# Norms between sub-layers of a two-layer decoder: old root ahead of the residual add, quotient applied to products, transposes placed by hand

## The chip, the cores and the metric

The kernel runs on one core of a Trainium2 chip. The metric is device time in microseconds for one execution. Engines are named as in the profile: PE is TensorE (its weight loads are PEld), DVE is VectorE, ACT is ScalarE, POOL is GpSimd, SP is SyncE, which issues nearly all transfers. Each engine works through its instructions in a fixed order, and an instruction that waits holds up those behind it on the same engine.

## The reference: what is computed

Two decoder layers over 256 rows (tokens) of 1024 numbers, float32. Each layer has three sub-layers: a feed-forward part, a mixer (pooling in layer 0, dilated attention in layer 1), a second feed-forward part. Every sub-layer has a norm on its input and one on its output, ahead of the residual add:

```python
def rms_norm(x, gain):
    y = x * lax.rsqrt(jnp.mean(x * x, axis=-1, keepdims=True) + RMS_EPS) * gain

def swiglu(h, w_gate, w_up, w_down):
    return (jax.nn.silu(h @ w_gate) * (h @ w_up)) @ w_down

# for each layer, with its six gains g
f = swiglu(rms_norm(h, g[0]), w_gate[0], w_up[0], w_down[0])
h = h + 0.5 * rms_norm(f, g[1])
mix = mixer(rms_norm(h, g[2]))
h = h + rms_norm(mix, g[3])
f = swiglu(rms_norm(h, g[4]), w_gate[1], w_up[1], w_down[1])
h = h + 0.5 * rms_norm(f, g[5])
# behind layer 0: keys and values for layer 1, from a norm of h with a gain of its own
```

## The kernel before

**Tiles.** The 256 rows are two blocks of 128 (block 0 and block 1; `i` in the code). The residual stream `h[0]`, `h[1]` stays in SBUF. Every product in float32 is made of three: each operand is split into a rounded high part and the rest (`hl`: high on ACT, line 99 or 106; rest on DVE, line 100 or 107), and high x high, high x low and low x high are added up in PSUM (`proj_mm`, lines 129 to 141; `row_mm`, lines 143 to 150). A product of 512 columns is one PE instruction. The weights come from HBM as one stream in the order of use, 1 MB at a time; a "unit" is half of that once it is split.

**A feed-forward sub-layer** (`ffn`, lines 272 to 451) first takes the normed, transposed rows `aT` against the first 512 gate and 512 up columns: `acc_b`, for each block 24 products for the gate and 24 for the up (lines 395 to 400). Then come two `pair`s (lines 335 to 387), which make one column group with seven block products instead of eight, by sums of blocks (`Sums`, lines 210 to 245, holds those of the rows); of the four sums of weight blocks in each pair two are made on DVE (line 333) and two by accumulating transfers that POOL issues (line 331). Then a last group, and the down projection `acc_d` over 22 row groups of 128 (lines 433 to 450). The last six of these (`TAIL = 6`) are kept back, so that block 0 is finished first: its 36 products of the tail, then the join for block 0, then the 36 of block 1's tail (six units of six products), in whose shadow block 0's join runs. The pool mixer ends in the same way (`acc_w`, lines 617 to 629).

**The join between two sub-layers** is the class `Bound` (lines 453 to 480) in three steps, for each block:

- `first`: `post` (lines 181 to 195). ACT squares both halves of the output in PSUM and sums them (line 174), DVE adds the two sums (line 176), POOL takes the power -1/2 (line 178). DVE multiplies the output with its gain (line 188 or 190) and adds it, times the root, to `h` (line 193).
- `second`: `norm` (lines 250 to 261). The same again for the new `h`: squares (line 174), sum, root, the product with the next gain (line 255), and the scaling by the root, one half on DVE (line 256), one on ACT (line 258).
- `third`: `transposed` (lines 197 to 208): eight PE transposes (line 203, tiles `tp`), then two casts to the high part on ACT (line 205) and two subtractions on DVE (line 206) into `aT`. Where the next sub-layer has `Sums`, ACT copies the transposed rows (line 230) and DVE and ACT build the sums.

There are five such joins, in the profile `f` for the three behind a feed-forward part (f00, f01, f10) and `m` for the two behind a mixer (m0, m1): f00, m0, f01, f10, m1 in order of time. Behind f10 the next stage is the key projection (`kp`, lines 670 to 679), which reads other rows (`hk`, a norm of its own, lines 636 to 642), not the rows of this join. The kernel starts with a norm of x (lines 482 to 498).

**What sets the order.** Most of the order on each engine is made by a planner from estimated durations: an instruction that is written earlier goes first when, by the estimate, both could run. On PE too it chooses where among the products the transposes go. Within `tc.manual_schedule(engines=...)` the order on the named engines is that of the code. That holds for DVE and ACT at the start (line 485) and in the attention part, and for PE in the attention part (lines 782 to 830), where block 0's transposes are written at `go.third(0)` behind it. `tc.issue_after(ins)` lets the instructions of its block that run on the engine of `ins` come only behind `ins`.

Of the kernel before, what the change touches and what calls it, by code (L numbers as in the profile page):

```python
# [11 lines left out]
F32 = mybir.dt.float32  # L12
# [15 lines left out]
TAIL = 6  # L28
DMA_SUMS = (2, 3)
# [18 lines left out]
def trunk_kernel(ctx: ExitStack, tc: tile.TileContext, x, pos, gains, pscale, ws, wq, invf, amask, pmat, icnt, out):  # L48
# [76 lines left out]

    def mm(o, l, r, start, stop):
        nc.tensor.matmul(o, l, r, start=start, stop=stop)  # L127
# [42 lines left out]
    def rstd_of(halves, name):  # L170
        ss = st.tile([P, 2], F32, tag="ss", name=f"ss_{name}")
        for k in range(2):
            jk = sc1.tile([P, 512], BF16, tag="junk", bufs=1, name=f"jk_{name}{k}")
            nc.scalar.activation(jk, halves[k], AF.Square, scale=1.0 / 32.0, accum_out=ss[:, k : k + 1])
        ms = st.tile([P, 1], F32, tag="ms", name=f"ms_{name}")
        nc.vector.scalar_tensor_tensor(ms, ss[:, 0:1], EPS, ss[:, 1:2], op0=ALU.add, op1=ALU.add)
        rs = st.tile([P, 1], F32, tag="rs", name=f"rs_{name}")
        nc.gpsimd.tensor_tensor(rs, ms, nhalf, op=ALU.pow)
        return rs
# [67 lines left out]
    def row_rstd(i, name):  # L247
        return rstd_of([h[i][:, 0:512], h[i][:, 512:1024]], f"q{name}{i}")

    def norm(i, gain, name, rs=None, split=True):  # L250
        rs = row_rstd(i, name) if rs is None else rs
        y = sc4.tile([P, D], F32, tag="y", name=f"n_{name}{i}")
        for k in range(2):
            c = slice(k * 512, (k + 1) * 512)
            nc.vector.tensor_mul(y[:, c], h[i][:, c], gain[:, c])
        nc.vector.tensor_scalar_mul(y[:, 0:512], y[:, 0:512], rs)
        if split:
            nc.scalar.mul(y[:, 512:1024], y[:, 512:1024], rs)
        else:
            nc.vector.tensor_scalar_mul(y[:, 512:1024], y[:, 512:1024], rs)  # L260
        return y

    def pre(i, gain, aT, name):
        transposed(i, norm(i, gain, name), aT, name)
# [7 lines left out]
    def ffn(n, aT, sums, boundary, middle=None, late=None):  # L272
# [180 lines left out]
    class Bound:  # L453


        def __init__(self, n, post_idx, half, pre_idx, sums=False):
            self.n, self.half, self.idx = n, half, (post_idx, pre_idx)
            self.want, self.sums = sums, None

# [17 lines left out]
        def __call__(self, i, f):  # L477
            self.first(i, f)
            self.second(i)
            self.third(i)  # L480

    gpre = load_gain(0, "pre")
    aT = new_aT("x")
    sums = Sums("x")
    with tc.manual_schedule(engines={mybir.EngineType.DVE, mybir.EngineType.Activation}):
        y = norm(0, gpre, "x")
# [4 lines left out]
        rs = row_rstd(1, "x")  # L491
        load_raw(at=1, raw=raws[0])
        first_units += [parts(raws[0], 1, xy=True)]
        y = norm(1, gpre, "x", rs, False)
# [38 lines left out]
    go = Bound("f00", 1, True, 2)  # L533
# [3 lines left out]
    aT = go.aT  # L537
    go = Bound("m0", 3, False, 4, True)
# [16 lines left out]
    def u_proj(i, n):  # L555
        proj_mm(uu[i][n], aT, i, units[n * 4 : n * 4 + 4], 512)
        d = u_hl[i][:, :, n * 512 : (n + 1) * 512]
        nc.scalar.copy(d[:, 0], uu[i][n])
        nc.vector.tensor_sub(d[:, 1], uu[i][n], d[:, 0])
# [38 lines left out]
    u_proj(0, 1)  # L598
# [21 lines left out]
    for i in range(2):  # L620
# [5 lines left out]
        else:  # L626
            for k in range(8 - TAIL, 8):
                wout(k, i)
        go(i, f[i])

    prev, go = go, Bound("f01", 5, True, 6, True)
    ffn(1, prev.aT, prev.sums, go)
# [3 lines left out]
    def kv_input():  # L636
        kvgain = load_gain(12, "post")
        hk.append(new_aT("hk"))
        for i in range(2):
            with in_turn("dve"):  # L640
                y = norm(i, kvgain, "kv")
            transposed(i, y, hk[0], "kv")

    prev, go = go, Bound("f10", 7, True, 8)
    ffn(2, prev.aT, prev.sums, go, None, kv_input)
# [3 lines left out]
    aT = go.aT  # L649
    go = Bound("m1", 9, False, 10, True)  # L650
# [19 lines left out]
    for g in range(3):  # L670
        units = load_units(4, g % 2 == 0)
        for i in range(2):
            ps = gup.tile([P, 512], F32, tag="gu", name=f"kp{g}{i}")
            proj_mm(ps, hkT, i, units, 512)
# [107 lines left out]
    with tc.manual_schedule(engines={mybir.EngineType.PE}):  # L782
# [44 lines left out]
        go.second(0)  # L827
        o_proj(1, (2,))
        values(3, 1)
        o_proj(1, (3,))  # L830
# [13 lines left out]
    ffn(3, go.aT, go.sums, Finish())  # L844
# [117 lines left out]
```

## Time and profile before

| what | value |
|---|---|
| median of 3 runs | 984.6 us (982.15 to 986.87) |
| the profiled execution | 985.76 us |
| its span | 984.0 us |
| mean granted clock of TensorE | 0.986 |
| instructions | 12092 |
| moved from HBM over the span | 178.54 MB read, 183 GB/s |
| longest wait of PE for another engine | 3.8 us, at the start (`tp_x` for `n_x`) |

How to read it: the page gives the busy time of every engine, and the chain that ended last is followed back from the last instruction to what released each step. In a list of groups a row is line, engine, operation, output<-inputs, count, then busy time and the mean time of one in ns, then idle time of the engine just before. In a timeline a row is start and length in us, engine, line, operation, tiles, shape, count of merged instructions, and in brackets the idle time ahead and what ended it. In the busy times by stretch each engine has its busy us and its count of instructions, in the order PE, PEld, DVE, ACT, POOL, then the granted clock, the share of the transfers' engines and GB/s.

### The profile page before, as it was taken

How to read it: one execution, taken by the hardware profiler on the slowest of the kernel's cores; microseconds unless marked ns; L12 is line 12 of the kernel's file. 1: busy time of each engine (PE TensorE's matmuls, PEld its weight loads, DVE VectorE, ACT ScalarE, POOL GpSimd, SP SyncE). 2: the span in 40 equal slices, each digit the busy share in tenths (PEclk: the TensorE clock that was granted, in tenths of full speed). 3: DMA queues.
4: the chain of work that ended last, by engine and by line, in shares of the span. 5: the costliest groups of instructions: out<-in, count | busy, mean ns of one | idle time of the engine just before them, and what ended most of it. 6: DMA issues, size and time to landing. Idle time of an engine off the chain costs nothing.

```text
span 984.0 us, 12092 instructions
## 1 busy us (share of the span) xinstructions
PE 950.4 (97%) x4560; PEld 783.7 (80%) x4560; DVE 684.1 (70%) x771; ACT 542.9 (55%) x693; POOL 62.3 (6%) x66
## 2 busy tenths in 40 slices
PE   7999999999999999999999999999987899999997
PEld 6888788878788878877888888788976778887886
DVE  5979874577788886458887964785465587887642
ACT  6665753455657565347656743644345576665531
POOL 0000000000100000000000000100033310000000
PEclk8999999999999999999999999999999799999999
DMA  7886876475468687546687765564324236967721
GB/s 248 286 266 205 259 260 207 173 227 187 164 211 265 181 280 261 179 139 213 153 317 218 268 243 175 177 217 139 127 95 153 86 107 194 330 163 260 247 90 43
DMA packets 55898, 197.16 MB, mean 200 GB/s; under 512 B 7392, under 2 KB 7392, under 8 KB 53792
## 3 DMA queue, kind: packets, MB, share of 16 engines
q1 hardware_dynamic: 53456, 179.35, 52.2%
q0 software_dynamic: 2384, 17.04, 8.9%
q8 instruction: 36, 0.59, 0.2%
q14 instruction: 22, 0.18, 0.0%
HBM read 178.54 MB, written 1.05 MB: 183 GB/s over the span
## 4 chain that ended last, share of the span: by engine, by line
PE 74%; DVE 11%; ACT 5%; DMA 4%; issue 3%; POOL 2%; SPq 0%; POOLq 0%; DVEq 0%; ACTq 0%
PE acc_d L127 22%; PE g L127 12%; PE st L314 12%; PE u L127 7%; PE acc_b L127 6%; PE vp L127 3%; DVE hl L100 3%; PE kp L127 3%; DMA xy<-raw 2%; DVE hl_lo L107 2%; PE htp L295 2%; ACT hl L99 2%; PE qp L127 1%; DVE h L193 1%; PE acc_w L127 1%
## 5 line engine op out<-in xcount | busy, mean ns | idle before, releaser
L100 DVE TENSOR_TENSOR hl<-raw,hl 128x1024 fp32r<-128x1024 f32 x182 | 221.0, 1222 | 111.6 <-ACT hl L99 110.5
L99 ACT CAST hl<-raw 128x1024 fp32r<-128x1024 f32 x182 | 189.7, 1051 | 138.3 <-PE acc_d L127 103.3
L127 PE MATMUL acc_d<-hl,h 128*128 128x512 f32 x1056 | 243.5, 390 | 0.0
L127 PEld LDWEIGHTS acc_d<-hl,h 128*128 128x128 f32 x1056 | 197.3, 188 | 40.4
L107 DVE TENSOR_TENSOR hl_lo<-xy,hl_hi 128x2048 fp32r<-128x2048 f32 x40 | 91.6, 2291 | 48.6 <-ACT hl_hi L106 48.6
L107 DVE TENSOR_TENSOR hl_lo<-raw,hl_hi 128x2048 fp32r<-128x2048 f32 x48 | 109.4, 2285 | 15.6 <-ACT hl_hi L106 15.5
L106 ACT CAST hl_hi<-xy 128x2048 fp32r<-128x2048 f32 x40 | 76.5, 1913 | 64.0 <-DVE xy L333 29.7
L106 ACT CAST hl_hi<-raw 128x2048 fp32r<-128x2048 f32 x48 | 91.9, 1914 | 20.8 <-PE st L314 10.6
L127 PE MATMUL acc_b<-hl,aT_m 128*128 128x512 f32 x192 | 44.8, 392 | 0.3 <-ACT aT_m L205 0.3
L127 PEld LDWEIGHTS acc_b<-hl,aT_m 128*128 128x128 f32 x192 | 35.7, 188 | 8.3 <-ACT aT_m L205 0.8
L127 PE MATMUL g<-hl_hi,aT_m 128*128 128x512 f32 x128 | 41.9, 393 | 0.0
L127 PE MATMUL u<-hl_hi,aT_m 128*128 128x512 f32 x128 | 41.8, 393 | 0.0
L314 PE MATMUL st<-hl_hi,S_m 128*128 128x512 f32 x128 | 41.8, 393 | 0.0
L127 PE MATMUL qp<-hl,aT_f 128*128 128x384 f32 x192 | 38.9, 354 | 0.0
L297 ACT CAST h<-htp 128x512 fp32r<-128x512 f32 (+1 forms) x48 | 26.2, 548 | 20.0 <-PE htp L295 20.0
L127 PEld LDWEIGHTS qp<-hl,aT_f 128*128 128x128 f32 x192 | 34.8, 198 | 1.3 <-issue 0.8
L127 PE MATMUL kp<-hl,aT_hk 128*128 128x512 f32 x144 | 34.6, 394 | 0.0
L331 POOL DMA_DIRECT2D xy<-raw x16 | 14.1, 878 | 305.2 <-DVE xy L333 82.3
L127 PE MATMUL vp<-hl,aT_hk 128*128 128x512 f32 x144 | 33.1, 390 | 0.0
L314 PE MATMUL st<-hl_hi,aT_m 128*128 128x512 f32 x96 | 31.6, 393 | 1.3 <-ACT hl L99 0.9
L721 POOL TENSOR_SCALAR p<-p,rd 128x512 f32<-128x512 f32 x16 | 24.9, 1566 | 121.9 <-DVE rd L720 100.1
L298 DVE TENSOR_TENSOR h<-htp,h 128x512 fp32r<-128x512 f32 (+1 forms) x48 | 30.6, 640 | 1.1 <-ACT h L297 1.0
(246 smaller groups left out, 1596.4 us busy)
## 6 DMA issues: line engine op xcount, KB each, us to landing
raw<-in_ws SPq DMA_DIRECT2D x278, 512.0 KB, 4.8
xy<-in_ws SPq DMA_DIRECT2D x32, 512.0 KB, 6.8
xy<-raw POOLq DMA_DIRECT2D x16, 1024.0 KB, 8.1
rawq<-in_wq SPq DMA_DIRECT2D x8, 768.0 KB, 4.7
gain_post<-in_gains SPq DMA_DIRECT2D x14, 256.0 KB, 5.0
gain_pre<-in_gains SPq DMA_DIRECT2D x12, 256.0 KB, 6.1
rawpm<-in_pmat SPq DMA_DIRECT2D x2, 512.0 KB, 4.1
out_dram<-h SPq DMA_DIRECT2D x4, 256.0 KB, 2.1
```

Source lines behind the costliest of these rows:

```text
L99: nc.scalar.copy(hl[:, 0, :n], raw[:, k, :n])
L100: last["dve"] = nc.vector.tensor_sub(hl[:, 1, :n], raw[:, k, :n], hl[:, 0, :n])
L106: nc.scalar.copy(hi, raw)
L107: last["dve"] = nc.vector.tensor_sub(lo, raw, hi)
L127: nc.tensor.matmul(o, l, r, start=start, stop=stop)
L193: nc.vector.scalar_tensor_tensor(h[i][:, c], y[:, c], rs, h[i][:, c], op0=ALU.mult, op1=ALU.add)
L295: nc.tensor.transpose(tp[:, k], prod[c, i][:, k * P : (k + 1) * P], ident)
L297: nc.scalar.copy(d[:, 0], tp[:, :nt])
L298: nc.vector.tensor_sub(d[:, 1], tp[:, :nt], d[:, 0])
L314: nc.tensor.matmul(ps, a(z, k), u[v], start=start and k == 0 and n == 0, stop=k == 3 and n == 2, skip_group_check=not start,)
L331: nc.gpsimd.dma_start(dst, src, accum_op=ALU.add)
L721: nc.gpsimd.tensor_scalar_mul(p, p, rd)
```

## The change

The rows that are transposed are no longer fully normed. Let r be the inverse root of the rows at the join before (`old`) and h the rows behind the residual add. Now each half of h is, directly behind its own residual add (`post` calls `done`, here `scaled`), multiplied by r and by the next gain in one DVE instruction. These rows are transposed. The true inverse root of h is obtained beside it: with m the mean square of h, `q = (m r r)^(-1/2)` is the quotient of new and old root, and `r q` the new root for the next join. The quotient is a factor per row, so it is applied behind the products: as the scale of the gate's SiLU and as a factor in the up product (`ffn`), as the scale of the pool mixer's copies (`u_proj`), and into the rope tables of the queries once the keys are done. The key/value norm takes the kept root and makes none of its own.

`Bound.first` now holds the residual add and these rows, `second` the transposes, `third` the squares, the quotient and the sums. `second` and `third` are put on a list and run at a hand-set mark: for block 0 behind the fourth of the six units of block 1's tail (`TURN_0 = 3`), for block 1 in the next stage behind the first unit of its second half (`TURN_1 = 0`): in `ffn` the first up unit of block 0, in the pool mixer that of block 0's second half, in the key projection the first unit of block 1. In the attention part block 0's `second` is written behind `values(3, 1)`.

The diff, without the unchanged lines around and without what only passes names along:

```diff
+TURN_0, TURN_1 = 3, 0
...
+    waiting = []
     def mm(o, l, r, start, stop):
-        nc.tensor.matmul(o, l, r, start=start, stop=stop)
+        last["mm"] = nc.tensor.matmul(o, l, r, start=start, stop=stop)
+
+    def run_waiting():
+        while waiting:
+            with tc.issue_after(last["mm"].ins):
+                waiting.pop(0)()
...
-    def norm(i, gain, name, rs=None, split=True):
-        rs = row_rstd(i, name) if rs is None else rs
+    def norm(i, gain, name, rs):
         y = sc4.tile([P, D], F32, tag="y", name=f"n_{name}{i}")
         for k in range(2):
             c = slice(k * 512, (k + 1) * 512)
-            nc.vector.tensor_mul(y[:, c], h[i][:, c], gain[:, c])
-        nc.vector.tensor_scalar_mul(y[:, 0:512], y[:, 0:512], rs)
-        if split:
-            nc.scalar.mul(y[:, 512:1024], y[:, 512:1024], rs)
-        else:
-            nc.vector.tensor_scalar_mul(y[:, 512:1024], y[:, 512:1024], rs)
+            nc.vector.scalar_tensor_tensor(y[:, c], h[i][:, c], rs, gain[:, c], op0=ALU.mult, op1=ALU.mult)
         return y
...
         def gate(c, i, g):
-            nc.scalar.activation(act[c, i][:, :w], g, AF.Silu)
+            nc.scalar.activation(act[c, i][:, :w], g, AF.Silu, scale=1.0 if q is None else q[:, i : i + 1])
         def up(c, i, u):
-            nc.vector.tensor_mul(prod[c, i][:, :w], u, act[c, i][:, :w])
+            if q is None:
+                nc.vector.tensor_mul(prod[c, i][:, :w], u, act[c, i][:, :w])
+            else:
+                nc.vector.scalar_tensor_tensor(
+                    prod[c, i][:, :w], u, q[:, i : i + 1], act[c, i][:, :w], op0=ALU.mult, op1=ALU.mult
+                )
...
             if n > 0:
                 proj_mm(gu[i][0], aT, i, units[:4], 512)
-                proj_mm(gu[i][1], aT, i, units[4:], 512)
+                for j in range(4):
+                    proj_mm(gu[i][1], aT, i, units[4:], 512, only=j)
+                    if j == TURN_1:
+                        run_waiting()
...
                 for t in range(TAIL):
                     down(NF - TAIL + t, i, tail[t])
+                    if t == TURN_0:
+                        run_waiting()
             boundary(i, f[i])
...
         def first(self, i, f):
-            post(i, f, self.gpost, self.half, self.n)
+            self.y = []
+            def scaled(i, c):
+                if not self.y:
+                    self.y.append(sc4.tile([P, D], F32, tag="y", name=f"n_{self.n}{i}"))
+                nc.vector.scalar_tensor_tensor(
+                    self.y[0][:, c], h[i][:, c], self.old[:, i : i + 1], self.gpre[:, c], op0=ALU.mult, op1=ALU.mult
+                )
+            post(i, f, self.gpost, self.half, self.n, scaled)
         def second(self, i):
-            self.y = norm(i, self.gpre, self.n)
+            transposed(i, self.y[0], self.aT, self.n, self.sums)
         def third(self, i):
-            transposed(i, self.y, self.aT, self.n, self.sums)
+            z, old = slice(i, i + 1), self.old[:, i : i + 1]
+            ms = mean_square(h_halves(i), f"q{self.n}{i}")
+            nc.vector.scalar_tensor_tensor(ms, ms, old, old, op0=ALU.mult, op1=ALU.mult)
+            nc.gpsimd.tensor_tensor(self.q[:, z], ms, nhalf, op=ALU.pow)
+            nc.gpsimd.tensor_mul(self.r[:, z], self.q[:, z], old)
             if self.sums is not None:
                 self.sums.add(i)
         def __call__(self, i, f):
             self.first(i, f)
-            self.second(i)
-            self.third(i)
+            def rest():
+                self.second(i)
+                self.third(i)
+            waiting.append(rest)
...
+    for i in range(2):
+        for t in (ctab, stab):
+            nc.vector.tensor_scalar_mul(t[:, i], t[:, i], qu[:, i : i + 1])
...
         p_turn(3, 1)
-        go.second(0)
         o_proj(1, (2,))
         values(3, 1)
+        go.second(0)
         o_proj(1, (3,))
     go.third(0)
     go(1, acc_f[1])
```

More of the change, by code (lines that the diff above doesn't have):

```diff
@@ L485, in trunk_kernel @@
     with tc.manual_schedule(engines={mybir.EngineType.DVE, mybir.EngineType.Activation}):
[L486 removed]
+        y = norm(0, gpre, "x", rstd_of(h_halves(0), "qx0", rx[:, 0:1]))
         raws = [load_raw(at=0)]
@@ L553, in trunk_kernel, with u_proj @@
     uu = [acc_pair(f"u{i}") for i in range(2)]
-    def u_proj(i, n):
-        proj_mm(uu[i][n], aT, i, units[n * 4 : n * 4 + 4], 512)
+    def u_proj(i, n, turn=False):
+        for q in range(4):
+            proj_mm(uu[i][n], aT, i, units[n * 4 : n * 4 + 4], 512, only=q)
+            if turn and q == TURN_1:
+                run_waiting()
         d = u_hl[i][:, :, n * 512 : (n + 1) * 512]
-        nc.scalar.copy(d[:, 0], uu[i][n])
-        nc.vector.tensor_sub(d[:, 1], uu[i][n], d[:, 0])
+        nc.scalar.mul(d[:, 0], uu[i][n], qu[:, i : i + 1])
+        nc.vector.scalar_tensor_tensor(
+            d[:, 1], uu[i][n], qu[:, i : i + 1], d[:, 0].bitcast(F32), op0=ALU.mult, op1=ALU.subtract
+        )
     yT = [s8p.tile([P, 2, 4, S], F32R, tag="s8", name=f"yT{k}") for k in range(2)]
@@ L673, in trunk_kernel @@
             ps = gup.tile([P, 512], F32, tag="gu", name=f"kp{g}{i}")
-            proj_mm(ps, hkT, i, units, 512)
+            for q in range(4):
+                proj_mm(ps, hkT, i, units, 512, only=q)
+                if i == 1 and q == TURN_1:
+                    run_waiting()
             r = rope(ps, i, 8, f"k{g}{i}")
```

52 lines of the change are left out of this document (29 added, 23 removed).

## The prediction

> **What bounds the kernel now.** I read the page first: the busy shares and the chain that ended last.
>
> ```profile
> PE 950.4 (97%) x4560; PEld 783.7 (80%) x4560; DVE 684.1 (70%) x771; ACT 542.9 (55%) x693; POOL 62.3 (6%) x66
> PE 74%; DVE 11%; ACT 5%; DMA 4%; issue 3%; POOL 2%; SPq 0%; POOLq 0%; DVEq 0%; ACTq 0%
> ```
>
> TensorE (PE) is busy for 97% of the span and carries 74% of the chain. Its speed inside a stage comes from the chain in order of time, its spare room from the busy times by stretch: one feed-forward sub-layer, then two stretches around a join between sub-layers.
>
> ```profile
> 61.72 5.44 PE u L127 x24
> 20.00:190.00 170.00, 168.96 (x764) 139.29 (x765) 125.64 (x123) 95.35 (x96) 3.63 (x4) 1.00 0.74 243
> 190.00:212.00 22.00, 20.84 (x99) 16.51 (x98) 18.45 (x28) 14.42 (x27) 3.98 (x4) 1.00 0.61 187
> 434.00:458.00 24.00, 22.19 (x105) 17.60 (x104) 20.22 (x31) 18.73 (x38) 3.06 (x4) 1.00 0.39 132
> ```
>
> Twenty-four 512-column products take 5.44 us, so one slot is 0.227 us. From 20 to 190 us PE is busy for 168.96 of 170.00 us; around the joins it is 20.84 of 22.00 and 22.19 of 24.00, and DVE is at 18.45 and 20.22. So the joins hold the idle time. PE's own waits say for what:
>
> ```profile
> PE tp_f L203 <- DVE n_f L256: 3.8, 6, 0.8
> PE tp_m L203 <- DVE n_m L256: 1.9, 3, 0.8
> PE acc_b L127 <- ACT aT_m L205: 0.3, 1, 0.3
> PE acc_u L127 <- ACT aT_f L205: 0.3, 1, 0.3
> PE acc_b L127 <- ACT aT_f L205: 0.3, 1, 0.3
> L127 PE MATMUL acc_d<-hl,h 128*128 128x512 f32 x1056 | 243.5, 390 | 0.0
> ```
>
> Nine waits of the transposes for the normed rows cost 3.8 + 1.9 = 5.7 us, and three of the next products for the transposed rows 0.9 us. The recorded end of a product is modelled: the last row gives 390 ns to one, whose slot is 227 ns, so every such wait hides another 0.163 us. Twelve waits: 6.6 + 12 x 0.163 = 8.6 us. That, and something at the start, is all that this change can win from waits.
>
> The timeline of the join after the first sub-layer, block 0 (rows 0 to 127), shows how a wait arises:
>
> ```profile
> 182.62 14.44 PE L127 MATMUL acc_d<-hl,h 128*128 128x512 f32 x63
> 190.14 0.60 ACT L174 ACTIVATE jk_pf<-acc_d 128x512 bf16<-128x512 f32 x1 [3.45 <-PE acc_d L127]
> 191.10 0.56 POOL L178 TENSOR_TENSOR rs_pf<-ms_pf,nhalf 128x1 f32<-128x1 f32 x1 [89.74 <-DVE ms_pf L176]
> 191.70 1.42 DVE L193 SCALAR_TENSOR_TENSOR h<-y_f,rs_pf,h 128x512 f32<-128x512 f32 x2
> 193.03 1.29 DVE L255 TENSOR_TENSOR n_f<-h,gain_pre 128x512 f32<-128x512 f32 x2
> 195.44 1.22 DVE L100 TENSOR_TENSOR hl<-raw,hl 128x1024 fp32r<-128x1024 f32 x1
> 195.60 1.47 POOL L178 TENSOR_TENSOR rs_qf<-ms_qf,nhalf 128x1 f32<-128x1 f32 x1 [3.94 <-DVE ms_qf L176]
> 197.10 0.72 ACT L258 ACTIVATE n_f<-n_f,rs_qf 128x512 f32<-128x512 f32 x1 [1.33 <-POOL rs_qf L178]
> 197.10 0.49 DVE L256 TENSOR_SCALAR n_f<-n_f,rs_qf 128x512 f32<-128x512 f32 x1 [0.44 <-POOL rs_qf L178]
> 197.73 1.99 ACT L99 CAST hl<-raw 128x1024 fp32r<-128x1024 f32 x2
> 197.74 1.06 PE L203 MATMUL tp_f<-ident,n_f 128*128 128x128 f32 x8 [0.67 <-DVE n_f L256]
> 199.62 1.06 ACT L205 CAST aT_f<-tp_f 128x512 fp32r<-128x512 f32 x2
> 200.25 8.50 PE L127 MATMUL acc_u<-hl,aT_f 128*128 128x512 f32 x36 [0.29 <-ACT aT_f L205]
> ```
>
> Down the rows: the last squares of the sub-layer's output (190.14), its inverse root (191.10), the residual add (191.70), the products with the gain (193.03), then squares of the new rows and a second root (195.60), the scaling (197.10), the transposes (197.74). They idle 0.67 us; the copies aT (199.62) stand behind two weight casts (197.73), and the next stage idles 0.29 us.
>
> **The change, part by part.** *The second root leaves the chain.* Now the gained rows h*gain end at 193.03 + 1.29 = 194.32, the transposes begin at 197.74: 3.42 us for the mean square, root and scaling. After, each half of h is at once multiplied by old root and gain in one DVE instruction. Its price is the one of the residual add, which has the same three operands:
>
> ```profile
> L193 DVE SCALAR_TENSOR_TENSOR h<-y_f,rs_pf,h 128x512 f32<-128x512 f32 x12 | 8.5, 748 | 0.8 <-POOL rs_pf L178 0.2
> ```
>
> 748 ns beside 1.29/2 = 0.65 us in the pair above; four such in a row from 191.70 end at 191.70 + 4 x 0.75 = 194.7, with overlap (1.42 for two) at 194.5. The rows are ready 3.0 us earlier than now.
>
> *Block 0's transposes by hand: behind the fourth of six units of block 1's tail.* Block 1's tail begins at about 190.06 (the squares start at 190.14, one semaphore step after the product); four units are 24 slots, 5.44 us: 195.5. Ready at 194.5 to 194.7, so no wait, with 0.8 us in hand. Behind them stand two units, 12 slots or 2.72 us, and the transposes' own 1.06 us: 3.8 us for two aT copies (1.06 us) and even the two casts of 1.99. So both waits of block 0 should go. The other three joins that have them at this place:
>
> ```profile
> 255.05 1.09 PE L203 MATMUL tp_m<-ident,n_m 128*128 128x128 f32 x8 [0.63 <-DVE n_m L256]
> 440.92 1.06 PE L203 MATMUL tp_f<-ident,n_f 128*128 128x128 f32 x8 [0.73 <-DVE n_f L256]
> 627.32 1.07 PE L203 MATMUL tp_f<-ident,n_f 128*128 128x128 f32 x8 [0.72 <-DVE n_f L256]
> ```
>
> 0.67 + 0.63 + 0.73 + 0.72 = 2.75, with the 0.9 of the three aT waits and 7 x 0.163: 4.8 us, bounds 3.4 (without the 0.9 + 3 x 0.163, the copies still late) to 4.8. I take 4.6. The attention join turns block 0 ahead of the last output product; it has no such wait now, and by its PE order gets none: 0.
>
> *Block 1's transposes by hand: behind 24 + 6 = 30 slots of the next stage, where the planner now puts 36.* This is the term I know least. Rows of two joins:
>
> ```profile
> 200.57 0.61 ACT L174 ACTIVATE jk_pf<-acc_d 128x512 bf16<-128x512 f32 x1
> 202.09 0.61 ACT L174 ACTIVATE jk_pf<-acc_d 128x512 bf16<-128x512 f32 x1
> 204.04 1.41 DVE L193 SCALAR_TENSOR_TENSOR h<-y_f,rs_pf,h 128x512 f32<-128x512 f32 x2
> 208.94 1.06 PE L203 MATMUL tp_f<-ident,n_f 128*128 128x128 f32 x8 [0.20 <-DVE n_f L256]
> 443.42 8.52 PE L127 MATMUL acc_b<-hl,aT_f 128*128 128x512 f32 x36 [0.28 <-ACT aT_f L205]
> 445.27 1.09 ACT L230 COPY sum_f<-tp_f 128x512 f32<-128x512 f32 x2
> 448.36 1.42 DVE L193 SCALAR_TENSOR_TENSOR h<-y_f,rs_pf,h 128x512 f32<-128x512 f32 x2
> 452.74 1.06 PE L203 MATMUL tp_f<-ident,n_f 128*128 128x128 f32 x8 [0.80 <-DVE n_f L256]
> ```
>
> Block 1's five waits are 5.7 - 2.75 = 2.95 us idle, with 5 x 0.163: 3.8 us. In the first join the tail ended at 200.25 - 0.29 - 0.163 = 199.80; the mark is 199.80 + 30 x 0.227 = 206.6. If ACT and DVE keep their order, h begins at 204.04, the rows end 1.41 + 1.29 later, plus 0.15 to PE (197.10 + 0.49 to 197.74): 206.9, a wait of 0.3. In the third join the tail ended at 443.42 - 0.28 - 0.163 = 442.98, the mark is 449.8, the rows are ready at 448.36 + 1.42 + 1.29 + 0.15 = 451.2: a wait of 1.4. Mean 0.85, times five 4.2: no gain at all, a loss of 0.4. But the order won't stay. In block 1 the two squares are 1.5 us apart (200.57, 202.09), with a cast between; in the third join the copies for the summed products (445.27, 1.09 us) stand between. Those belong to block 0's transposes, which move from 197.74 to about 195.5, so that aT and sum copies (1.06 + 1.09) lie ahead of the tail's end. With ACT free there, block 0's own steps give the chain: one square more (0.61), 191.70 - 190.14 = 1.56 to h, 2.85 to the rows and PE: 5.0 us behind the tail's end, where the mark is at 6.8. One cast more (half of the 1.99 at 197.73) still fits. So between -0.4 and +3.8; nearer the free case, since what stood between leaves; I take 2.6.
>
> *The start.* There is no manual mark, but the scaling behind the gain product goes.
>
> ```profile
> 9.91 0.72 ACT L258 ACTIVATE n_x<-n_x,rs_qx 128x512 f32<-128x512 f32 x1 [4.85 <-DVE n_x L255]
> 10.54 1.03 ACT L99 CAST hl<-raw 128x1024 fp32r<-128x1024 f32 x1
> 16.02 1.28 DVE L255 TENSOR_TENSOR n_x<-h,gain_pre 128x512 f32<-128x512 f32 x2
> ```
>
> ACT loses 0.72 us at 9.91; but the cast at 10.54 may have to wait for its weights all the same, so block 0 gains 0 to 0.7. Block 1 loses 1.28 + 2 x 0.49 us of DVE from 16.02 (gain products at 0.64, and two scalings of the 0.49 at 197.10 behind them) and gets two of 0.75: about 0.7. I take 0.6, bounds 0 to 1.2.
>
> *What is added.* Per block a small DVE product, POOL's root and a POOL product with the old root, behind the transposes. The first to wait is the gate (ACT), behind 24 slots, 5.4 us, of the next stage. If it waited, the casts queued on ACT behind it would, and PE behind those. In the first join h of block 0 is there at 191.70 + 1.42 = 193.1 and such a gate would come at 199.8 + 5.4 = 205.2: 12 us of cover for two squares, root and product of 2 x 0.6 + 2 x 1.5 us; so 0. Query tables get their factor by four small DVE products, under 0.49 us each (197.10 is larger), while the value projections, which read no table, run: 0. Gates, up products and the pool mixer's copies now take a per-row factor: at most the 0.72 of 9.91 where a plain copy takes half of 1.06 (199.62), 0.2 us each. It lies on PE's path where PE waits for such a copy, in the mixer and where a transpose follows an up product: two of them, 0.4 us, bounds 0 to 1 (five). The key/value norm loses its own squares and roots, which no PE wait above names: 0.
>
> A rule speaks against one of these. POOL's root took 0.56 us at 191.10, and 1.47 at 195.60 beside the cast remainder of 195.44, a DVE instruction with two SBUF inputs. The Trainium skill says on the page "SBUF — State Buffer", section "Who interferes with whom", that a VectorE instruction with two SBUF inputs contends with a GpSimd one that reads SBUF, and that issue order decides who waits; the trace agrees on POOL's side, and by that rule the new POOL product of block 0 could stop DVE for its own length ahead of block 1's rows. At the 0.56 us of 191.10 that is five times 0.56, 2.8 us, and the sum would be 4.6 (980.0), close to the first rival below. No row shows DVE stopped (1.22 us at 195.44 beside 1.47 of POOL), and DVE has 1.8 us in hand there (6.8 - 5.0), so I leave the sum as it is and count the rule in that rival's chance.
>
> Sum: 4.6 + 2.6 + 0.6 - 0.4 = 7.4 us. The profiled execution took 985.76 us (span 984.0 and 1.8 around), so 978.4; the median of the three runs is 984.6, 1.2 lower, so **977.2 us**.
>
> **The rivals.** *Only block 0 counts:* the new mark for block 1 is too early and the saved wait comes back there (the order-as-now sum, -0.4). Then 4.6 - 0.4 + 0.6 - 0.4 = 4.4 us: 980.2. For it: DVE's 20.22 of 24.00 us at such a join leaves little air. Against: the removed instructions.
>
> *The planner doesn't follow the marks:* they only forbid an earlier place. If it thinks the rows late, transposes stay where they are; the chain is still 3 us shorter, so block 0's waits go and block 1 wins about 1: 4.6 + 1 + 0.6 - 0.4 = 5.8, 978.8.
>
> *PE is not the bound:* weights arrive at their own pace (DMA share 0.74, 243 GB/s from 20 to 190), and PE would only wait later. Then only part of the start stays, 0 to 1 us: 984. Against it: PE idles 1.04 us in those 170. The Trainium skill ("Perfetto Trace Analysis", section "Identifying the Most-Contended Engine") holds that the matmul share is no measure of headroom and the weight-load share is; this page has 80% there, so by the rule a fifth is free. The slot of 0.227 us that never shortens while inputs are ready speaks against taking that as room the joins could not use.
>
> *Slower, by ACT's order:* block 0's second squares (two of 0.6, no longer needed early) and one more cast (1.0) are put ahead of block 1's first squares: 2.2 us on the chain of each block 1. The wait there becomes 0.85 + 2.2 = 3.05, times five 15.2, where now 3.8 is lost: 11.4 lost, 4.8 won otherwise (4.6 + 0.6 - 0.4): 6.6 slower, 991.2. It decides from (3.8 + 4.8)/5 - 0.85 = 0.87 us of such work per block. Against it: these squares can run as soon as h exists, at 193.1 where the tail ends at 199.8.
>
> **How the numbers follow.** Forecast 0.62; only block 0 0.13; marks not followed 0.07; PE not the bound 0.10; ACT's order 0.08. About 0.5%, 4.9 us, is what a measurement of this kernel can tell from no change. The forecast's own terms run from 3.4 - 0.4 + 0 - 1 = 2.0 to 4.8 + 3.8 + 1.2 = 9.8 us. Of its 0.62 I put 0.60 above 4.9; of the first rival (4.4) 0.04, of the second (5.8) 0.04: faster 0.68. Slower is ACT's order, 0.08; the rest, 0.24, is the same. The range goes from 974.8 (9.8 won) to 982.6 (2.0 won), which leaves out the last two rivals, 0.18.
>
> **What would show it.** In the profile after, the waits of tp_f and tp_m for DVE should fall from 5.7 to under 1.5 us in total, those for aT to nothing; the transposes of block 0 should be followed by 12 products of the tail; those of block 1 should come behind 30. If the waits fall and the time doesn't, later waits took it, and the third rival holds. If tp waits of block 1 exceed 0.9 us each, block 1's term failed; if squares of h stand on ACT directly ahead of block 1's squares of the output, the slower one holds.

## The result, and the profile after

| | before | after |
|---|---|---|
| median | 985.12 us of 4 runs (982.15 to 986.87) | 971.6 us of 4 runs (969.83 to 972.42) |
| span of the profiled execution | 984.0 us | 970.7 us |
| ratio | | 0.9864, 95% interval 0.9846 to 0.9882 |

The change makes the kernel 13.5 us faster. That is the direction of the forecast, but 5.6 us below its 977.2 and 3.2 us below the lower end of its range. First the page of the changed kernel, the two lines that were read first in the one before: busy time by engine, and shares of the chain that ended last.

```profile
PE 946.7 (98%) x4560; PEld 784.5 (81%) x4560; DVE 682.6 (70%) x768; ACT 536.3 (55%) x672; POOL 62.7 (6%) x74
PE 92%; DVE 3%; ACT 2%; issue 1%; DMA 1%; POOL 0%; SPq 0%; DVEq 0%; POOLq 0%; ACTq 0%
```

PE carried 74% of that chain before and carries 92% now; DVE fell from 11% to 3%. Next the busy times by stretch, the same stage and the same two joins (the later ones begin earlier, as time was saved ahead of them); columns as before.

```profile
20.00:190.00 170.00, 168.96 (x765) 139.22 (x764) 125.54 (x123) 95.15 (x96) 3.63 (x4) 1.00 0.75 244
189.00:211.00 22.00, 22.00 (x107) 18.41 (x106) 17.86 (x28) 13.25 (x25) 3.50 (x6) 1.00 0.57 180
427.00:451.00 24.00, 24.00 (x116) 20.05 (x115) 22.50 (x36) 17.29 (x32) 3.50 (x6) 1.00 0.42 142
```

The inner stretch has not moved at all: 168.96 us of 170. Both joins are full, 22.00 of 22.00 and 24.00 of 24.00. The list of what PE waits for confirms it; these are all of its lines for the transposes of normed rows or for their copies:

```profile
PE tp_x L216 <- DVE n_x L267: 3.4, 2, 2.1
PE acc_b L130 <- ACT aT_x L218: 1.3, 1, 1.3
```

Both belong to the start. The lines for `tp_f` and `tp_m`, 5.7 us before, and the three for `aT_f` and `aT_m` are gone (the attention part has waits of its own, before and after). The timeline of the join after the first sub-layer shows the steps of the change in place, without PE's weight loads:

```profile
191.93 1.42 DVE L206 SCALAR_TENSOR_TENSOR h<-y_f,rs_pf,h 128x512 f32<-128x512 f32 x2
192.77 0.63 ACT L183 ACTIVATE jk_qf<-h 128x512 bf16<-128x512 f32 x1
193.26 1.41 DVE L489 SCALAR_TENSOR_TENSOR n_f<-h,r_x,gain_pre 128x512 f32<-128x512 f32 x2
...
195.55 1.03 PE L216 MATMUL tp_f<-ident,n_f 128*128 128x128 f32 x8
...
196.34 2.98 PE L130 MATMUL acc_d<-hl,h 128*128 128x512 f32 x12
...
199.16 6.97 PE L130 MATMUL acc_u<-hl,aT_f 128*128 128x512 f32 x30
...
199.78 1.04 ACT L100 CAST hl<-raw 128x1024 fp32r<-128x1024 f32 x1
...
200.72 0.60 ACT L183 ACTIVATE jk_pf<-acc_d 128x512 bf16<-128x512 f32 x1
201.12 1.22 DVE L101 TENSOR_TENSOR hl<-raw,hl 128x1024 fp32r<-128x1024 f32 x1
...
204.40 1.41 DVE L489 SCALAR_TENSOR_TENSOR n_f<-h,r_x,gain_pre 128x512 f32<-128x512 f32 x2
...
205.97 1.03 PE L216 MATMUL tp_f<-ident,n_f 128*128 128x128 f32 x8
```

Block 0's gained rows are ready at 193.26 + 1.41 = 194.67, the transposes start at 195.55 with nothing to wait for, and 12 tail products follow (x12). Block 1's rows are ready at 204.40 + 1.41 = 205.81 and their transposes come at 205.97, behind 30 products (x30): just in time. Four joins have 30 there; in the key projection the planner went past the mark, to 43.

**Where 13.3 us of span went.** What a wait costs PE can be counted from the start of one product to the start of the next, less the slot of 0.227 us (or a transpose's own, shorter one, where that stands ahead). By that count the twelve waits at the joins cost 8.5 us before (block 0's seven 4.8, block 1's five 3.7) and cost nothing now. That leaves nearly 5 us which no part of the prediction has. They are in the second of the two pairs of the feed-forward parts 1, 2 and 3, and at the start of the last group right behind it. PE stopped there eight times before the change, 4.2 us by the same count (0.36 + 1.05 + 0.61, 0.36 + 0.24, 0.38 + 0.60 + 0.57; the last of each part is in the last group), and never stops now. So 8.5 + 4.2 = 12.7 of 13.3 us have a place.

How such a pair looked before the change, in feed-forward part 1; first the timeline, without PE's running products:

```profile
328.58 2.29 DVE L107 TENSOR_TENSOR hl_lo<-xy,hl_hi 128x2048 fp32r<-128x2048 f32 x1 [1.37 <-ACT hl_hi L106]
...
331.39 2.29 DVE L333 TENSOR_TENSOR xy<-xy,raw 128x2048 f32<-128x2048 f32 x1
...
334.51 2.28 DVE L107 TENSOR_TENSOR hl_lo<-raw,hl_hi 128x2048 fp32r<-128x2048 f32 x1
...
336.86 5.17 SPq L91 DMA_DIRECT2D raw<-in_ws  x4
...
341.82 0.86 POOL L331 DMA_DIRECT2D xy<-raw  x1 [13.82 <-DMA raw<-in_ws]
```

Then the chain in order of time for that stretch (start, length, what), and PE's two largest stops of this part from the timeline:

```profile
337.23 4.03 DMA raw<-in_ws
...
341.82 12.20 DMA xy<-raw
...
354.13 1.92 ACT hl_hi L106
```

```profile
359.11 0.47 PE L314 MATMUL st<-hl_hi,aT_m 128*128 128x512 f32 x1 [0.89 <-ACT hl L99]
...
368.85 1.40 PE L127 MATMUL g<-hl,aT_m 128*128 128x512 f32 x5 [0.40 <-DVE m L289]
```

Read it as one chain. DVE makes the second sum of weight blocks (331.39, `xy<-xy,raw`) ahead of the split of the gate block (334.51, `hl_lo<-raw`). The split ends at 336.80, and only then is the buffer of that block free, so SP's next weight load goes out at 336.86. It lands at 341.26; POOL's accumulating transfer for the fourth sum, which needs that block, is issued at 341.82 and takes 12.20 us. ACT's cast of the result (354.13) is late, the splits behind it are late, and PE stops at 359.11 and, in the last group, at 368.85. (The first stop of the part, 0.36 us at 336.85, is a gate product that waits for the late split itself.)

The same place after the change:

```profile
326.12 2.29 DVE L108 TENSOR_TENSOR hl_lo<-xy,hl_hi 128x2048 fp32r<-128x2048 f32 x1 [1.12 <-ACT hl_hi L107]
...
328.33 2.29 DVE L108 TENSOR_TENSOR hl_lo<-raw,hl_hi 128x2048 fp32r<-128x2048 f32 x1
...
331.13 2.28 DVE L342 TENSOR_TENSOR xy<-xy,raw 128x2048 f32<-128x2048 f32 x1
...
337.98 0.86 POOL L340 DMA_DIRECT2D xy<-raw  x1 [12.84 <-DVE hl_lo L108]
```

The split (328.33) now stands ahead of the sum (331.13). The first row of each fence is the split of the sum before it; from there the accumulating transfer is 341.82 - 328.58 = 13.24 us away before and 337.98 - 326.12 = 11.86 after, and it no longer waits for a weight load. It also takes 10.04 us in place of 12.20, so its result is there 3.5 us sooner. PE does not stop in this stretch. Nothing in the diff names this order. It is the planner's, and the change has altered something by which it decides.

One more order has turned, on PE itself. Before the change the last group of each of these parts has its first four transposes (`htp`) ahead of its first product; that is where PE stopped for `m` at 368.85. After it, two stand behind the first six products (363.75) and two behind the next six (365.36). This is part of the 4.2 us too.

### The profile page after: what moved, and what is told of

It reads as the page before. It is cut to its first block, busy times and chain, and to the rows that moved or that the text cites. A ratio compares the mean times of both kernels' runs of the same rounds, so it can differ in the third digit from the quotient of the medians.

```text
span 970.7 us, 12064 instructions
## 1 busy us (share of the span) xinstructions
PE 946.7 (98%) x4560; PEld 784.5 (81%) x4560; DVE 682.6 (70%) x768; ACT 536.3 (55%) x672; POOL 62.7 (6%) x74
## 3 DMA queue, kind: packets, MB, share of 16 engines
HBM read 178.54 MB, written 1.05 MB: 185 GB/s over the span
## 4 chain that ended last, share of the span: by engine, by line
PE 92%; DVE 3%; ACT 2%; issue 1%; DMA 1%; POOL 0%; SPq 0%; DVEq 0%; POOLq 0%; ACTq 0%
PE acc_d L130 24%; PE st L323 15%; PE g L130 13%; PE u L130 9%; PE acc_b L130 9%; PE kp L130 3%; PE vp L130 3%; PE qp L130 3%; PE acc_w L130 2%; PE acc_u L130 2%; PE htp L304 2%; PE ob L130 1%; DVE hl L101 1%; DMA raw<-in_ws 1%; PE acc_o L130 1%
## 5 line engine op out<-in xcount | busy, mean ns | idle before, releaser
L130 PEld LDWEIGHTS vp<-hl,aT_hk 128*128 128x128 f32 x144 | 27.0, 188 | 5.6
```

What stands on the lines that cost most here:

```text
L130: last["mm"] = nc.tensor.matmul(o, l, r, start=start, stop=stop)
```

## The experiments

Four things were asked: whether the order in the pairs is worth what the count says, what turned it, what the marks are worth apart from the shorter chain, and whether anything is left. "Pair order" below means where the second sum stands to the split of the gate block in the second pair of parts 1 to 3.

### 1. The kernel before, with the sum held behind the split

```diff
-            add(x, z, 1)
+            with in_turn("dve") if n > 0 else nullcontext():
+                add(x, z, 1)
```

> The kernel before, with one edge more: in the pairs of the three later feed-forward parts DVE's second sum of weight blocks (line 333, xy<-xy,raw) may only come behind the split of the block that is written ahead of it; only the three last pairs change their order by it, to the order of the kernel after. Theory (the joins gave 8.6 us, and some 4 us came from these pairs, because the planner now puts the sum behind the split, so that a buffer for the next block is free earlier): 985.1 - 4 = 981, and PE's waits in those pairs (at about 359, 369, 895, 905 us) are gone while the waits of the joins stay. Rival (these waits went because everything arrives earlier from the joins, the order doesn't matter): 985, waits stay.

Measured: 980.32 us (977.46 to 982.06, 8 runs), before beside it 983.48; ratio 0.9966, interval 0.9951 to 0.9981, so 3.3 us faster, 1.9 to 4.8. PE's waits and the pair of this kernel:

```profile
PE tp_f L203 <- DVE n_f L256: 3.8, 6, 0.8
PE tp_m L203 <- DVE n_m L256: 1.9, 3, 0.8
```

```profile
330.81 2.29 DVE L107 TENSOR_TENSOR hl_lo<-raw,hl_hi 128x2048 fp32r<-128x2048 f32 x1 [0.55 <-ACT hl_hi L106]
...
333.62 2.28 DVE L333 TENSOR_TENSOR xy<-xy,raw 128x2048 f32<-128x2048 f32 x1
```

The join waits stand untouched at 3.8 and 1.9 us. Of the eight stops the three at the start of the last groups are left, at about 0.24 us each, since PE's own order there is still the old one; the other five are gone. By the count that is 3.5 us. So the pair order alone is worth about 3 us, and it has nothing to do with the joins.

### 2. The kernel before, with the up product in its new form and a factor of one

```diff
+    ones = cp.tile([P, 1], F32, name="ones")
+    nc.gpsimd.memset(ones, 1.0)
...
-            nc.vector.tensor_mul(prod[c, i][:, :w], u, act[c, i][:, :w])
+            if n == 0:
+                nc.vector.tensor_mul(prod[c, i][:, :w], u, act[c, i][:, :w])
+            else:
+                nc.vector.scalar_tensor_tensor(
+                    prod[c, i][:, :w], u, ones[:, 0:1], act[c, i][:, :w], op0=ALU.mult, op1=ALU.mult
+                )
```

> The kernel before, with the up product of the three later feed-forward parts as one instruction with a per-row factor, as in the kernel after, but the factor is 1; nothing else is changed. Theory (it is this form, by its estimate alone, that makes the planner put the second sum behind the split): 981, as with the order set by hand, minus at most 0.5 us for the 0.06 us that each of 72 such products takes longer off PE's path. Rival (the form costs DVE time and gives nothing): 985 to 987.

Measured: 980.09 us (978.99 to 980.51), ratio 0.996, interval 0.9945 to 0.9975. The pair again:

```profile
331.57 2.28 DVE L109 TENSOR_TENSOR hl_lo<-raw,hl_hi 128x2048 fp32r<-128x2048 f32 x1
...
334.38 2.28 DVE L340 TENSOR_TENSOR xy<-xy,raw 128x2048 f32<-128x2048 f32 x1
```

Split first, sum second. Nothing was moved by hand: the multiplication by one, an instruction that only costs more, turned the planner's order in all three pairs, and the transposes of the last groups with it, and gained 3.9 us by the ratio (2.5 to 5.4; 3.4 between the medians). All eight stops are gone; a new one of 1.15 us appeared in the first pair of part 3. The text ahead of the run speaks of 72 such products; there are 36 in the three parts.

### 3. The changed kernel, with the sum put back ahead of the split

```diff
-            us = load_form()
+            early = n > 0 and c == 3
+            raw = load_raw()
+            if early:
+                add(x, z, 1)
+            us = form(raw, early)
...
-            add(x, z, 1)
+            if not early:
+                add(x, z, 1)
```

With the second argument set, `form` holds its split behind the sum on DVE.

> The kernel after, with the second sum put ahead of the split in the second pair of the three later feed-forward parts, the order of the kernel before. Theory: PE's waits in those pairs come back, 971.6 + 4 = 975.6, the joins stay without waits. Rival (earlier joins took these waits away, not the order): 971.6.

Measured: 976.56 us (974.76 to 978.45), ratio 0.9925, interval 0.9909 to 0.9941, against 971.6 for the changed kernel. PE stops in the three pairs again; two of the stops of part 1:

```profile
332.52 0.51 PE L131 MATMUL g<-hl_lo,aT_m 128*128 128x512 f32 x1 [0.35 <-DVE hl_lo L109]
...
354.28 0.47 PE L324 MATMUL st<-hl_hi,aT_m 128*128 128x512 f32 x1 [0.38 <-DVE c L386]
```

Eight stops cost 3.9 us by the count, no join waits. They are not the same eight: the first two of each pair cost 0.96 us together where one cost 0.36, and none is left in the last groups, whose transposes stay where the change has them. This kernel is about the change as the prediction had it, with the pairs nearly as they were, and its time is 0.6 us from the 977.2 that was forecast. That it is so near is in part luck: block 1's term was too small, the start's too large (below).

### 4. The changed kernel without marks

```diff
-            waiting.append(rest)
+            rest()
```

> The kernel after, without the two marks: transposes, squares, quotient and sums are written directly behind the residual add, as before, and the planner places them. Theory A (the shorter chain is what counts, the planner finds about the same places): 971.6 to 973, no waits of tp for DVE over 0.5 us. Theory B (the planner's estimate of the chain is too short by 0.7 to 1.0 us as it was before, so that it places the transposes too early again and the marks are what removes the waits): 4 to 8 us slower, 976 to 980, with nine waits of 0.5 to 0.9 us.

Measured: 974.79 us (973.58 to 975.39), ratio 0.9907, interval 0.989 to 0.9924: 3.2 us slower than the changed kernel, 2.2 slower than its second set of runs (972.64, below; the two intervals overlap). That lies between the two theories. The planner alone puts block 0's first transposes in front of 20 tail products, not 12, and block 1's behind 26, not 30 (22 in the last join):

```profile
193.75 0.63 PE L216 MATMUL tp_f<-ident,n_f 128*128 128x128 f32 x4 [0.26 <-DVE n_f L489]
...
194.81 4.62 PE L130 MATMUL acc_d<-hl,h 128*128 128x512 f32 x19
```

PE waits in seven places, 2.6 us by the count: four times for block 0's rows (1.6 us together), and for block 1's in the key projection and in the last join (1.0). Behind 26 products in the other three joins block 1's transposes wait for nothing. So the marks are worth two to three us, and by doing the opposite of what one expects of them: the planner places transposes ahead of the time at which their rows are ready, as it did before the change, and the mark holds them back.

### 5. The shorter chain alone: no marks, and the old pair order

> The kernel after without both other things: no marks (the planner places the transposes), and the second sum of weight blocks ahead of the split in the three last pairs, as before. What is left of the change is the shorter chain and what hangs on it. Theory that the three parts add up: the marks were worth 3.2 us, the order 3.2 to 5.0, so 971.6 + 6.4 to 8.2 = 978 to 980, which leaves 4 to 6 us for the chain. Rival (marks and order win the same time twice, since both only let PE arrive at the same later wait): 975 to 977.

The edits are those of 3 and 4 together. Measured: 978.97 us (974.52 to 982.73), ratio 0.9948, interval 0.9931 to 0.9965. So the shorter chain with what hangs on it is worth 5.1 us, 3.4 to 6.9: the gates and up products still have their factor, and the last groups' transposes their new places. The joins lose 2.9 us by the count where they lost 8.5; the pairs lose 4.4, and 1.3 more go at the key/value transposes of experiment 8. With the marks (2 to 3) and the pair order (4 to 5) this adds up to 11 to 13 us; measured for all together 11 to 13.5. The parts add up, and the rival (975 to 977) is outside the interval.

### 6. Both marks one unit later

```diff
-TURN_0, TURN_1 = 3, 0
+TURN_0, TURN_1 = 4, 1
```

> The kernel after with both marks six products later (behind the fifth unit of block 1's tail; behind the second unit of the half that follows). Theory (a mark only has to lie behind the rows and far enough ahead of the next stage; block 0 still has 6 products and its transposes, 2.4 us, for two copies of 1.06 us and a cast of 1.0): 971.6, at most 1 us more if a second cast stands ahead of the copies. Rival (the marks are at the one right place): 3 us slower or more, with waits for aT back at 0.3 us or more each.

Measured: 970.84 us (969.9 to 971.77), ratio 0.9865, interval 0.985 to 0.988: not to be told from the changed kernel. Block 0's transposes now have six tail products behind them, block 1's come behind 36, where the kernel before had them in three of five joins (33 and 31 in the others):

```profile
197.13 1.62 PE L130 MATMUL acc_d<-hl,h 128*128 128x512 f32 x6
...
198.58 8.69 PE L130 MATMUL acc_u<-hl,aT_f 128*128 128x512 f32 x36
```

The rows had been ready long before (203.82 + 1.41 = 205.23 in this execution). The joins' only cost was 0.2 us in each of three, for DVE's half of block 0's `aT`. So for block 1 the place behind 30 won nothing over 36.

### 7. Every pair with the sum behind the split, in the changed kernel

```diff
-            add(x, z, 1)
+            with in_turn("dve"):
+                add(x, z, 1)
```

> The kernel after, with the second sum behind the split in the first pair of the first feed-forward part too, the only one of eight that the planner still orders the other way. Theory: that pair has no wait of PE, so nothing to win there: 971.6; if its buffers being free earlier also takes away the wait of 1.2 us at about 100 us, 970.4.

Measured: 971.13 us (969.26 to 973.24), ratio 0.9865, interval 0.9848 to 0.9882. It turns the one pair that had the sum first after the change too, the first of part 0, and gains nothing there, since PE does not stop in that pair. The order is worth something only where the late load runs into PE's need. The stop that part 0 does have, about 1.18 us in its second pair, stays in every kernel of this study.

### 8. The changed kernel again, and the key/value transposes

> The kernel after, unchanged, on the chip of the three runs below, so that they have a common base: 971.6 again.

Measured: 972.64 us (969.88 to 975.45), ratio 0.989, interval 0.9871 to 0.9909. Its profiled execution has a wait that the first profile shows at 0.04 us:

```profile
555.14 1.05 ACT L100 CAST hl<-raw 128x1024 fp32r<-128x1024 f32 x1 [1.88 <-DMA raw<-in_ws]
...
559.25 1.25 PE L216 MATMUL tp_kv<-ident,n_kv 128*128 128x128 f32 x8 [1.70 <-DVE aT_hk L219]
```

A weight block came 1.88 us late to ACT (555.14; its transfer took 5.8 us, 4.2 in the first profile), the copies of the first key/value transposes stand behind it, and the second transposes, only 8 products later, wait 1.70 us. The profiles of experiments 5, 6 and 7 have the same wait, 1.1 to 1.8 us. It is not what sets the two sets of runs apart: the execution that shows it is the fastest of its six (969.88), and the first profile, without it, the slowest of its four (972.42). The next kernel holds these back until behind the third row group:

```diff
-            transposed(i, y, hk[0], "kv")
+            if i == 0:
+                transposed(i, y, hk[0], "kv")
+            else:
+                waiting.append(lambda: transposed(1, y, hk[0], "kv"))
...
             down(c, 1, units[c % 2])
+            if n == 2 and c == 2:
+                run_waiting()
```

> The changed kernel with one more hand-set place: the four transposes of block 1's key/value rows (tile tp_kv, the second group) go behind the third row group of the following down projection, about 36 products of 0.227 us after the first group, where they stood after 8. Theory: what the repeated runs of the changed kernel lose there (1.70 us idle at 559.25, in other executions 0.2) is a wait for the buffer that the copies of the first group hold, which stand on ACT behind weight casts; 8 us of room takes it away in every execution. Then no wait of tp_kv remains and the median is 970 to 971.6 us beside 971.6 to 972.6 for the changed kernel, 0.2 to 1.7 lower. Rival: the wait is a late arrival of weights that stops PE anyway at the next product; then tp_kv's wait goes, products idle there by the same amount, and the time stays at 971.6 to 972.6.

Measured: 970.62 us (968.81 to 971.63), ratio 0.986, interval 0.9842 to 0.9878. The median is inside the first bounds, but the trace is not:

```profile
559.13 0.44 PE L304 MATMUL htp<-ident,m 128*128 128x128 f32 x2 [0.89 <-DVE aT_hk L219]
```

No transpose of the key/value rows waits, but another transpose, `htp` of the last column group, stops for the same copy, 0.89 us. The weight block is as late as before (1.97 us at 555.01), and whichever transposes come next wait for the copies behind it on ACT; the wait was partly handed on. A difference of 1 to 2 us between medians whose runs spread over 3 us and more settles nothing. All small moves together:

> The same with all the small moves together: the key/value transposes held back, block 0's transposes behind the fifth of six units in place of the fourth, the second sum of weight blocks behind the split in every pair. If the room before block 0's transposes and the order of the pairs are both without cost, as measured one by one (970.8 and 971.1), this comes to 969.5 to 971 us. Rival: block 0's transposes, with 6 products of cover left for their copies, stop the next stage by 0.2 us in three joins as they did with both marks late, and the sum stays at 971 to 972.

Measured: 970.79 us (968.3 to 973.85), ratio 0.9868, interval 0.9847 to 0.9889. The 0.2 us stops of the rival are there in three joins; the median can't tell the two apart. None of these versions is measurably faster than the change itself.

## Why the prediction was right and wrong

**The sum of the waits** was the step that failed: "That, and something at the start, is all that this change can win from waits." The 8.6 us were counted at the joins, and the inner stretch was judged from one window, 20 to 190 us, where PE idles 1.04 us. That window is feed-forward part 0, the one part whose second pair had the split first already. The waits of parts 1 to 3 stood in the same list of PE's waits, in these lines:

```profile
PE st L314 <- ACT hl L99: 0.9, 1, 0.9
PE g L127 <- DVE m L289: 0.8, 2, 0.4
PE g L127 <- DVE hl_lo L107: 0.6, 3, 0.2
PE st L314 <- DVE c L371: 0.4, 1, 0.4
```

They are 2.7 us of idle time, 4.2 by the count from start to start, and the prediction doesn't weigh them: no edit touches those instructions. But the edit to the up product changes an instruction that the planner places on the same engine, and experiment 2 shows that this alone turns the order. Experiments 1, 2 and 3 give it 3.3, 3.9 and 4 to 5 us; the trace has 4.2, of which experiment 1 leaves 0.7 that belong to the transposes of the last groups. The missed 5.6 us are mostly this; the rest is block 1's term, 1.1 too small, less the start's.

**Block 0's term**, 4.6 with bounds 3.4 to 4.8, was 4.8 us: all seven waits went. The rows came at 194.67 where 194.5 to 194.7 was worked out.

**Block 1's term**, 2.6 with bounds -0.4 to 3.8, was 3.7 us, near its upper end. The reasoning was looser than the result. It had the rows 5.0 us behind the tail's end, with ACT free, and 1.8 us in hand. They came 205.81 - 199.16 = 6.65 us behind it: a weight cast still stands between the two squares on ACT (199.78), and a cast's remainder on DVE ahead of their sum (201.12). The 1.8 us in hand were used up to 0.16, and the wait went all the same. Going earlier than 36 had no part in it: 36 does as well (experiment 6).

**"The planner doesn't follow the marks"** supposed that marks only forbid earlier places and that the planner might think the rows late. The first half is right (in the key projection the transposes went past the mark); the second is the other way round. It places them early, and the marks bind (experiment 4).

**The start**, 0.6 with bounds 0 to 1.2, gave nothing: the first product begins at 12.59 us after and at 12.11 before. The other profiled kernels with the changed start lie between 11.2 and 12.1, those with the start of before between 10.7 and 11.9, so the start varies by more than the term. The step had named why it could be zero, the weights, and the next row of the changed kernel says so: the weight cast ahead of the first product waits for its transfer, and the copies `aT_x` stand behind it. In this execution the second half of the gained rows came late too: it waited 2.02 us for its gain's load, until 9.81.

```profile
11.01 1.04 ACT L100 CAST hl<-raw 128x1024 fp32r<-128x1024 f32 x1 [5.63 <-DMA raw<-in_ws]
```

**The added factors**, -0.4, cost PE nothing that the trace shows. They do cost their engines something, gates and up products alike; groups of the kernel before, then of the changed one:

```profile
L289 DVE TENSOR_TENSOR m<-c,s 128x512 f32<-128x512 f32 x16 | 11.0, 685 | 0.0
L284 ACT ACTIVATE s<-g 128x512 f32<-128x512 f32 x16 | 9.5, 591 | 9.0 <-PE g L127 9.0
```

```profile
L296 DVE SCALAR_TENSOR_TENSOR m<-c,q_m,s 128x512 f32<-128x512 f32 x8 | 6.0, 745 | 0.0
L288 ACT ACTIVATE s<-g,q_m 128x512 f32<-128x512 f32 x8 | 5.3, 685 | 0.1
```

0.745 in place of 0.685 us and 0.685 in place of 0.591. The rule about DVE and POOL is answered by rows of the first join after the change:

```profile
197.05 1.22 DVE L101 TENSOR_TENSOR hl<-raw,hl 128x1024 fp32r<-128x1024 f32 x1
...
197.22 1.46 POOL L502 TENSOR_TENSOR q_f<-ms_qf,nhalf 128x1 f32<-128x1 f32 x1 [5.33 <-DVE ms_qf L501]
...
198.76 0.19 POOL L503 TENSOR_TENSOR r_f<-q_f,r_x 128x1 f32<-128x1 f32 x1
...
209.20 0.55 POOL L502 TENSOR_TENSOR q_f<-ms_qf,nhalf 128x1 f32<-128x1 f32 x1 [6.17 <-DVE ms_qf L501]
```

DVE's cast remainder takes 1.22 us beside POOL's power (197.05) and 1.22 with POOL idle (201.12). The power takes 1.46 us beside the cast and 0.55 without one (209.20). POOL's new product, which the rule's sum put at 0.56, takes 0.19 here. The Trainium skill, "SBUF — State Buffer", section "Who interferes with whom", lets either side wait; the trace agrees on POOL's side and shows no wait on DVE's, and the 980.0 us by that rule did not come.

**The rivals.** Only block 0 counts: refuted, block 1 gave 3.7 us. ACT's order: block 0's second squares do stand ahead of block 1's, at 192.77, but six us before the tail ends, so they are not on the chain, as the prediction argued. PE is not the bound: refuted by the 8.5 us that turned into time. The Trainium skill's rule behind that rival ("Perfetto Trace Analysis", section "Identifying the Most-Contended Engine") judges TensorE's headroom by the share of peak operations (MFU) and the weight-load share. The latter is 81% after the change and 80% before; with PE on 92% of the chain, that share did not tell how much was left to win.

**Left open:** why the planner's estimate turns the order, on DVE and on PE, was not traced step by step, and 0.6 us of the 13.3 have no single place.

## What to carry to other kernels

Where a planner orders the instructions, a change of an instruction's form can change the order, also far from the edit: so before giving the waits that a change can win, list all waits of the bound engine, those in stretches that it doesn't touch too, and add those that hang on the order of an engine whose instructions get another form. A window judged as typical should be checked against its siblings; the one window here was the only one of four without the fault. And when a change makes work ready earlier, a planner may still place what waits for it too early: then a mark that holds it back is part of the gain; here it added about half of what the shorter chain gave alone.

## What the runs showed of the hardware

An accumulating transfer of 1 MB that POOL issues took from 6.9 to 12.2 us, and the longest ones in parts 1 and 3 (12.2 and 11.7) were among those issued late; after the change the same ones took 10.0 and 8.6. Lateness does not explain it alone: the late one of part 2 took 7.9, and one in part 0 that was in time took 11.4.

TensorE's granted clock falls to 0.50 of full speed for stretches of 3.4 or 6.8 us. Besides the last 3 us, the profile before and the one after each have four of them, one at the start (at 11.4 and 11.7 us) and three in the attention part, 23.8 us in all, and both have a mean of 0.986: so the 13.3 us between the two are not a matter of the clock. Experiment 8's profile has three, 10.2 us, and a mean of 0.993. Within one kernel the lower clock goes with the longer time: in that experiment 969.88 us at 0.993 and 975.45 at 0.984. This spread is larger than what experiments 6 to 8 were to tell apart.
